# A row-wise softmax on one core: which tile is loaded first, and from which queue

## The chip, the cores and the metric

The kernel runs on one core of a Trainium2 chip. The time is device microseconds of one execution. The program has five instruction streams: PE (TensorE), DVE (VectorE), ACT (ScalarE), POOL (GpSimd) and SP (SyncE). Transfers between the chip's memory and the core's on-chip buffer are made by 16 DMA engines; SyncE, ScalarE and GpSimd each issue transfers on a queue of their own. "Issue" is the instruction that starts a transfer, "landing" the moment at which its semaphore is complete.

## The reference: softmax with temperature 2

```python
x = np.random.randn(16, 1024, 512).astype(np.float32)
x_scaled = x / 2.0
x_max = np.max(x_scaled, axis=-1, keepdims=True)
exp_x = np.exp(x_scaled - x_max)
out = (exp_x / np.sum(exp_x, axis=-1, keepdims=True)).astype(np.float32)
```

Input and output are 16,384 rows of 512 floats, 33.55 MB each. The kernel leaves the maximum out of its main path: it takes exp(0.5 x) and the row sums at once, multiplies by the reciprocal of the sum, and counts at the end whether all row sums lie between 1.0 and 1e30. Only if one does not, a second path (the `rounds`, L142) computes everything again with the maximum. With this input it does not run.

## The kernel before, in words

**Rows and tiles.** The 16,384 rows are spread over 128 partitions, so that each partition holds 128 rows of 2 KB ("rows" below are these 128). `TILES` (L10) cuts them into ten tiles, each given as (rows, place in the arena): 3, then 5, then eight of 15. A tile is one transfer in and one transfer out, and in memory each partition's part of a tile is contiguous: 15 rows are 30,720 bytes, 5 rows 10,240, 3 rows 6144. The arena (L49) is the on-chip buffer, with room for 98 of the 128 rows; the work is done in place.

**Loads.** SyncE issues tile 0 and ScalarE tile 1 in `early` (L153). Their instructions are moved by L278 to L286 in front of the barrier with which all engines begin. Tile 1 is the `SPREAD` tile: its fifth row goes by itself, in one transfer of partitions 0 to 125 and one of partitions 126 and 127 (L117), so that its load is three transfers. Behind the barrier ScalarE issues tiles 2 to 7 (`loads`, L157), one after the other on its queue. Tiles 8 and 9 reuse rows of the arena: `LATE` (L14) names the tiles whose stores must have landed first. GpSimd issues them (L176 to L179), after it has waited until all exponentials of the rows below `TURN` are done, and then for the stores in `LATE`, in order.

**Computing.** TensorE waits for each tile's landing and passes it on as permits, one for each chunk (L194). ScalarE takes a permit for a chunk and does one activation for each row of it, with the row's sum as a by-product. The first chunk (`HEAD`, three rows) is written out straight (L201); the others have five rows and run in a loop with a register as row number (`exponentials`, L259). VectorE then does a reciprocal and one multiply (L163 to L173) for up to three chunks of a tile, and for one chunk at a time in the last tile.

**Stores and the end.** SyncE issues the stores in the order of the tiles (L211), each when its multiplies are done. The store of the last tile but one has a semaphore of its own, `s_near`. The three computing engines wait for it and for the count of row sums, read the flag and step over the second path (L142 to L151). SyncE waits for `s_near` and for all the other stores (L256, L257), which ends the program.

Of the kernel before, what the change touches and what calls it, by code (L numbers as in the profile page):

```python
# [7 lines left out]


TILES = [  # L10
    (3, 0), (5, 3), (15, 8), (15, 23), (15, 38), (15, 53), (15, 68), (15, 83), (15, 0), (15, 15),
]

LATE = {8: (0, 1, 2), 9: (3,)}  # L14
ARENA = 98

HEAD = [3]
E = 5

SPREAD = 1  # L20

TURN = 83

LO, HI = 1.0, 1.0e30
G = 64
# [3 lines left out]
def kernel(  # L29
# [5 lines left out]
    nc = tc.nc  # L35
# [3 lines left out]
    Exp = mybir.ActivationFunctionType.Exp  # L39
# [6 lines left out]
    n_rows = N // P  # L46
    assert sum(r for r, _ in TILES) == n_rows

    arena = nc.alloc_sbuf_tensor("arena", (P, ARENA, D), fp32)  # L49
    stats = nc.alloc_sbuf_tensor("stats", (P, n_rows), fp32)  # L50
# [10 lines left out]
    for r, at in TILES:  # L61
        assert at == base % ARENA
        tiles.append((base, r, at))
# [6 lines left out]
    def sb(t):  # L70
        _, r, at = tiles[t]
        return arena[:, at : at + r, :]

    straight = sum(HEAD)
    sizes = HEAD + [E] * ((n_rows - straight) // E)
    starts = [sum(sizes[:k]) for k in range(len(sizes))]
    assert sum(sizes) == n_rows
    owner = [max(t for t, (b, _, _) in enumerate(tiles) if b <= s) for s in starts]
# [12 lines left out]
    ld = [nc.alloc_semaphore(f"ld{t}") for t in range(len(tiles))]  # L91
    s_home = {t: nc.alloc_semaphore(f"s_home{t}") for t in LATE}
    s_near = nc.alloc_semaphore("s_near")
    s_end = nc.alloc_semaphore("s_end")
    s_exp = nc.alloc_semaphore("s_exp")
    s_go = nc.alloc_semaphore("s_go")
# [16 lines left out]
    def load(eng, t):  # L113
        r = tiles[t][1]
        parts = [(0, P, 0, r)]
        if t == SPREAD:
            parts = [(0, P, 0, r - 1), (0, 126, r - 1, r), (126, P, r - 1, r)]  # L117
        for p, q, lo, hi in parts:
            eng.dma_start(  # L119
                out=sb(t)[p:q, lo:hi], in_=dram(xf, t)[p:q, lo:hi]  # L120
            ).then_inc(ld[t], 16)

    stored_by = {u: s_home[t] for t, us in LATE.items() for u in us}
    for t, (_, r, at) in enumerate(tiles):
        over = {u for u, (_, ru, au) in enumerate(tiles[:t]) if at < au + ru and au < at + r}
        assert over <= {u for v, us in LATE.items() if v <= t for u in us}

    def landings(ts):
        return 16 * len(list(ts))
# [9 lines left out]
    def take(eng, sem, n):  # L139
        eng.wait_ge(sem, n).then_inc(sem, -n)  # L140
# [11 lines left out]

    def early():  # L153
        load(nc.sync, 0)
        load(nc.scalar, 1)

    def loads():  # L157
        for t in range(2, min(LATE)):
            load(nc.scalar, t)

    def program():

        for j, ks in enumerate(pairs):  # L163
            b, c = starts[ks[0]], sum(sizes[k] for k in ks)
            a = b % ARENA
            nc.vector.reciprocal(  # L166
                out=recip[:, b : b + c], in_=stats[:, b : b + c]
            )._wait_ge(s_exp, ks[-1] + 1).then_inc(s_rec, 1)
            nc.vector.tensor_mul(  # L169
                out=arena[:, a : a + c],  # L170
                in0=arena[:, a : a + c],
                in1=recip[:, b : b + c].unsqueeze(2).to_broadcast([P, c, D]),
            )._wait_ge(s_rec, j + 1).then_inc(s_mul, 1)  # L173

        nc.gpsimd.memset(ones[:, :], 1.0).then_inc(s_ones, 1)  # L175
        nc.gpsimd.wait_ge(s_exp, starts.index(TURN))  # L176
        for t, us in LATE.items():
            nc.gpsimd.wait_ge(s_home[t], landings(us))
            load(nc.gpsimd, t)  # L179
        nc.gpsimd.tensor_scalar(  # L180
            out=inside[:, :], in0=stats[:, :], scalar1=LO, scalar2=HI,
            op0=Alu.max, op1=Alu.min,
        )._wait_ge(s_exp, len(sizes)).then_inc(s_cnt, 1)
        nc.vector.scalar_tensor_tensor(  # L184
            out=inside[:, :], in0=inside[:, :], scalar=1.0, in1=stats[:, :],
            op0=Alu.mult, op1=Alu.is_equal, accum_out=count[:, :],
        )._wait_ge(s_cnt, 1).then_inc(s_cnt, 1)
        nc.vector.tensor_scalar(  # L188
            out=flag[:, :], in0=total[:, :], scalar1=float(N), scalar2=None, op0=Alu.is_ge,
        )._wait_ge(s_tot, 1).then_inc(s_flag, 1)  # L190


        for t in range(len(tiles)):
            nc.tensor.wait_ge(ld[t], 48 if t == SPREAD else 16).then_inc(s_go, owner.count(t))  # L194
        nc.tensor.wait_ge(s_ones, 1)
        nc.tensor.matmul(  # L196
            total[:, :], lhsT=count[:, :], rhs=ones[:, :], start=True, stop=True
        )._wait_ge(s_cnt, 2).then_inc(s_tot, 1)

        nc.scalar.preload_act_table(Exp)  # L200
        for k, c in enumerate(HEAD):  # L201
            take(nc.scalar, s_go, 1)
            for b in range(starts[k], starts[k] + c):
                ins = nc.scalar.activation(  # L204
                    out=arena[:, b], in_=arena[:, b], func=Exp, scale=0.5,
                    accum_out=stats[:, b : b + 1],
                )
            ins.then_inc(s_exp, 1)
        exponentials(straight, n_rows)

        for t in range(len(tiles)):  # L211
            store(nc.sync, t)

        x_g = xf.rearrange("(t p r) d -> t p r d", p=P, r=G)
        o_g = of.rearrange("(t p r) d -> t p r d", p=P, r=G)
        data = arena[:, 0:G]

        def vector():  # L220
            for i in range(n_rows // G):
                nc.vector.reduce_max(
                    out=g_max[:, :], in_=data, axis=mybir.AxisListType.X, negate=True
                )._wait_ge(g_go, i + 1).then_inc(g_top, 1)
                nc.vector.reduce_sum(
                    out=g_sum[:, :], in_=data, axis=mybir.AxisListType.X
                )._wait_ge(g_exp, i + 1).then_inc(g_add, 1)
                nc.vector.reciprocal(
                    out=g_sum[:, :], in_=g_sum[:, :]
                )._wait_ge(g_add, i + 1).then_inc(g_rec, 1)  # L230

        def scalar():
            for i in range(n_rows // G):
                nc.scalar.activation(out=data, in_=data, func=Exp, scale=0.5)._wait_ge(
                    g_sub, i + 1
                ).then_inc(g_exp, 1)

        def gpsimd():
            nc.gpsimd.wait_ge(s_end, at_end)
            for i in range(n_rows // G):  # L240
                nc.gpsimd.dma_start(out=data, in_=x_g[i]).then_inc(g_ld, 16)
                nc.gpsimd.wait_ge(g_ld, 16 * (i + 1)).then_inc(g_go, 1)
                nc.gpsimd.tensor_add(
                    out=data, in0=data, in1=g_max[:, :].unsqueeze(2).to_broadcast([P, G, D])
                )._wait_ge(g_top, i + 1).then_inc(g_sub, 1)
                nc.gpsimd.tensor_mul(
                    out=data, in0=data, in1=g_sum[:, :].unsqueeze(2).to_broadcast([P, G, D])
                )._wait_ge(g_rec, i + 1).then_inc(g_mul, 1)
                nc.gpsimd.wait_ge(g_mul, i + 1)
                nc.gpsimd.dma_start(out=o_g[i], in_=data).then_inc(g_st, 16)  # L250
                nc.gpsimd.wait_ge(g_st, 16 * (i + 1))

        rounds(nc.vector, vector)
        rounds(nc.scalar, scalar)
        rounds(nc.gpsimd, gpsimd)
        nc.sync.wait_ge(s_near, 16)  # L256
        nc.sync.wait_ge(s_end, at_end)  # L257

    def exponentials(first, end):  # L259
        row = nc.scalar.alloc_register(f"row{first}")  # L260
        nc.scalar.reg_mov(row, first)
        with nc.scalar.While(lambda: nc.scalar.snap(row, min_val=first, max_val=end) < end):
            now = nc.scalar.snap(row, min_val=first, max_val=end - E)
            take(nc.scalar, s_go, 1)
            at = nc.s_assert_within(
                now % ARENA, 0, ARENA - E,
                skip_runtime_bounds_check_because="no chunk reaches over the arena's end",
            )
            for r in range(E):
                data = arena[:, r : ARENA - E + 1 + r][:, bass.ds(at, 1)]  # L270
                ins = nc.scalar.activation(  # L271
                    out=data, in_=data, func=Exp, scale=0.5,
                    accum_out=stats[:, r : n_rows - E + 1 + r][:, bass.ds(now, 1)],
                )
            ins.then_inc(s_exp, 1)
            nc.scalar.reg_add(row, row, E)
# [45 lines left out]
```

## Time and profile before

| what | value |
|---|---|
| runs | 159.97, 167.96 and 169.0 us; median 167.96 us |
| profiled execution: its own span, first to last instruction | 158.7 us |
| bytes moved in it, loads / stores | 33.55 / 33.55 MB |
| busy: ACT / DVE / POOL | 80.8 / 73.2 / 2.2 us |
| stores on SyncE's queue: first and last issue | 10.9 and 143.7 us |
| last landing | 158.7 us |

The profile shows one execution. A busy time is that of instructions which compute; waiting, branching and issuing transfers are not counted. A queue (q1 is SyncE's, q10 ScalarE's, q0 GpSimd's) is worked off by all 16 DMA engines in the order of issue, and the queues run beside one another. A line of stretches gives, for each engine, its busy time in that stretch with the number of instructions, then the DMA engines' mean busy share and the bytes moved per time. Packets are timed from start to end, and two that overlap on an engine both count, so a share can be a little over 1.

### The profile page before, as it was taken

How to read it: one execution, taken by the hardware profiler on the slowest of the kernel's cores; microseconds unless marked ns; L12 is line 12 of the kernel's file. 1: busy time of each engine (PE TensorE's matmuls, PEld its weight loads, DVE VectorE, ACT ScalarE, POOL GpSimd, SP SyncE). 2: the span in 40 equal slices, each digit the busy share in tenths (PEclk: the TensorE clock that was granted, in tenths of full speed). 3: DMA queues.
4: the chain of work that ended last, by engine and by line, in shares of the span. 5: the costliest groups of instructions: out<-in, count | busy, mean ns of one | idle time of the engine just before them, and what ended most of it. 6: DMA issues, size and time to landing. Idle time of an engine off the chain costs nothing. (4 is left out here: it accounts for less than half of the span.)

```text
span 158.7 us, 657 instructions
## 1 busy us (share of the span) xinstructions
PE 0.2 (0%) x2; PEld 0.1 (0%) x2; DVE 73.2 (46%) x27; ACT 80.8 (51%) x257; POOL 2.2 (1%) x8
## 2 busy tenths in 40 slices
PE   0000000000000000000000000000000000000000
PEld 0000000000000000000000000000000000000000
DVE  0047001992981990059500991008932981992000
ACT  0590598697498008940399001991597009940000
POOL 0000000000000000000000300000000000010000
DMA  7999998989999999999999999999999999999995
GB/s 271 382 496 396 463 437 324 480 382 485 410 457 410 457 410 449 418 449 418 441 426 441 426 434 434 426 441 426 441 418 449 418 449 410 457 403 465 403 457 256
DMA packets 3024, 67.11 MB, mean 423 GB/s; under 512 B 336, under 2 KB 336, under 8 KB 720
## 3 DMA queue, kind: packets, MB, share of 16 engines
q1 hardware_dynamic: 1584, 34.34, 50.4%
q10 hardware_dynamic: 1152, 24.90, 37.1%
q0 software_dynamic: 288, 7.86, 11.5%
HBM read 33.55 MB, written 33.55 MB: 423 GB/s over the span
## 5 line engine op out<-in xcount | busy, mean ns | idle before, releaser
L271 ACT ACTIVATE arena<-arena x125 | 76.8, 615 | 54.1 <-ACTq L140 54.1
L169 DVE TENSOR_TENSOR arena<-arena,recip 128x7680 f32<-128x7680 f32 (+2 forms) x12 | 70.2, 5847 | 0.4
L166 DVE RECIPROCAL recip<-stats 128x15 f32<-128x15 f32 (+2 forms) x12 | 2.7, 224 | 70.4 <-ACT arena L271 61.4
L271 ACT ACTIVATION_READ_ACCUMULATOR arena<-arena x125 | 23.4, 187 | 0.0
L200 ACT ACT_TABLE_LOAD x1 | 1.3, 1283 | 5.7 <-issue 5.7
L119 POOL DMA_DIRECT2D arena<-in_x_dram x2 | 1.3, 638 | 84.9 <-ACT arena L271 84.9
L204 ACT ACTIVATE arena<-arena 128x512 f32<-128x512 f32 x3 | 1.9, 619 | 0.0
L180 POOL TENSOR_SCALAR inside<-stats 128x128 f32<-128x128 f32 x1 | 0.6, 630 | 51.7 <-ACT arena L271 51.7
L204 ACT ACTIVATION_READ_ACCUMULATOR arena<-arena 128x1 f32 x3 | 0.6, 188 | 0.0
L196 PE MATMUL total<-ones,count 128*1 128x1 f32 x2 | 0.2, 164 | 143.9 <-DVE inside L184 143.9
L184 DVE SCALAR_TENSOR_TENSOR inside<-inside,stats 128x128 f32<-128x128 f32 x1 | 0.3, 282 | 0.0
L188 DVE TENSOR_SCALAR flag<-total 1x1 int32<-1x1 f32 x1 | 0.1, 146 | 0.3 <-PE total L196 0.3
L196 PEld LDWEIGHTS total<-ones,count 128*1 128x1 f32 x2 | 0.1, 80 | 143.9 <-DVE inside L184 143.9
L175 POOL MEMSET ones<- 128x1 f32 x1 | 0.1, 98 | 2.2 <-POOLq L37 2.2
L306 POOL MEMSET const-bfloat16-1.0<- 128x1 bf16 x1 | 0.1, 108 | 0.0
L306 POOL MEMSET const-uint8-127<- 128x1 uint8 x1 | 0.1, 108 | 0.0
L306 POOL MEMSET const-float32-0.0<- 128x1 f32 x1 | 0.1, 104 | 0.2 <-issue 0.2
L306 POOL MEMSET const-float32-1.0<- 128x1 f32 x1 | 0.1, 104 | 0.0
L184 DVE DVE_READ_ACCUMULATOR inside<-inside,stats 128x1 f32 x1 | 0.1, 80 | 0.0
## 6 DMA issues: line engine op xcount, KB each, us to landing
out_dram<-arena SPq DMA_DIRECT2D x8, 3840.0 KB, 26.2
arena<-in_x_dram ACTq DMA_DIRECT2D x6, 3840.0 KB, 46.7
arena<-in_x_dram POOLq DMA_DIRECT2D x2, 3840.0 KB, 33.6
out_dram<-arena SPq DMA_DIRECT2D x1, 1280.0 KB, 22.9
arena<-in_x_dram ACTq DMA_DIRECT2D x1, 1024.0 KB
arena<-in_x_dram SPq DMA_DIRECT2D x1, 768.0 KB, 5.6
out_dram<-arena SPq DMA_DIRECT2D x1, 768.0 KB, 14.6
arena<-in_x_dram ACTq DMA_DIRECT2D x1, 252.0 KB
```

The lines of the kernel that those rows point to most:

```text
L119: eng.dma_start(out=sb(t)[p:q, lo:hi], in_=dram(xf, t)[p:q, lo:hi]).then_inc(ld[t], 16)
L166: nc.vector.reciprocal(out=recip[:, b : b + c], in_=stats[:, b : b + c])._wait_ge(s_exp, ks[-1] + 1).then_inc(s_rec, 1)
L169: nc.vector.tensor_mul(out=arena[:, a : a + c], in0=arena[:, a : a + c], in1=recip[:, b : b + c].unsqueeze(2).to_broadcast([P, c, D]),)._w ...
L175: nc.gpsimd.memset(ones[:, :], 1.0).then_inc(s_ones, 1)
L180: nc.gpsimd.tensor_scalar(out=inside[:, :], in0=stats[:, :], scalar1=LO, scalar2=HI, op0=Alu.max, op1=Alu.min,)._wait_ge(s_exp, len(sizes) ...
L184: nc.vector.scalar_tensor_tensor(out=inside[:, :], in0=inside[:, :], scalar=1.0, in1=stats[:, :], op0=Alu.mult, op1=Alu.is_equal, accum_ou ...
L188: nc.vector.tensor_scalar(out=flag[:, :], in0=total[:, :], scalar1=float(N), scalar2=None, op0=Alu.is_ge,)._wait_ge(s_tot, 1).then_inc(s_f ...
L196: nc.tensor.matmul(total[:, :], lhsT=count[:, :], rhs=ones[:, :], start=True, stop=True)._wait_ge(s_cnt, 2).then_inc(s_tot, 1)
L200: nc.scalar.preload_act_table(Exp)
L204: ins = nc.scalar.activation(out=arena[:, b], in_=arena[:, b], func=Exp, scale=0.5, accum_out=stats[:, b : b + 1],)
L271: ins = nc.scalar.activation(out=data, in_=data, func=Exp, scale=0.5, accum_out=stats[:, r : n_rows - E + 1 + r][:, bass.ds(now, 1)],)
L306: nc = _bacc.Bacc("TRN2", target_bir_lowering=False, num_devices=1)
```

## The change

The order of the tiles changes, and with it who loads what:

- The tiles are now six of 15 rows, one of 5, two of 15 and one of 3. The arena has 95 rows instead of 98. There are ten tiles as before.
- SyncE still issues tile 0 in front of the barrier; this is now a tile of 15 rows. ScalarE issues nothing there. Tiles 1 to 6 are issued by ScalarE behind the barrier.
- No tile is split: `SPREAD` is `None`.
- GpSimd issues three late loads instead of two: tiles 7, 8 and 9, which wait for the stores of tiles 0, 1 and 2, one each. `TURN` is 80 instead of 83; both are row numbers, and row 80 stands behind the first chunk of tile 5.
- The chunk of three rows is the last one (`TAIL`) instead of the first; its activations are written out straight behind the loop. `s_near` now belongs to the last tile of 15 rows (tile 8), and the store behind it has 3 rows.

```diff
 TILES = [
-    (3, 0), (5, 3), (15, 8), (15, 23), (15, 38), (15, 53), (15, 68), (15, 83), (15, 0), (15, 15),
+    (15, 0), (15, 15), (15, 30), (15, 45), (15, 60), (15, 75), (5, 90), (15, 0), (15, 15), (3, 30),
 ]
-LATE = {8: (0, 1, 2), 9: (3,)}
-ARENA = 98
-HEAD = [3]
+LATE = {7: (0,), 8: (1,), 9: (2,)}
+ARENA = 95
+TAIL = 3
 E = 5
-SPREAD = 1
-TURN = 83
+SPREAD = None
+TURN = 80
...
-    straight = sum(HEAD)
-    sizes = HEAD + [E] * ((n_rows - straight) // E)
+    turned = n_rows - TAIL
+    sizes = [E] * (turned // E) + [TAIL]
...
     def early():
         load(nc.sync, 0)
-        load(nc.scalar, 1)
     def loads():
-        for t in range(2, min(LATE)):
+        for t in range(1, min(LATE)):
             load(nc.scalar, t)
...
         nc.scalar.preload_act_table(Exp)
-        for k, c in enumerate(HEAD):
-            take(nc.scalar, s_go, 1)
-            for b in range(starts[k], starts[k] + c):
-                ins = nc.scalar.activation(
-                    out=arena[:, b], in_=arena[:, b], func=Exp, scale=0.5,
-                    accum_out=stats[:, b : b + 1],
-                )
-            ins.then_inc(s_exp, 1)
-        exponentials(straight, n_rows)
+        exponentials(0, turned)
+        take(nc.scalar, s_go, 1)
+        for b in range(turned, n_rows):
+            a = b % ARENA
+            ins = nc.scalar.activation(
+                out=arena[:, a], in_=arena[:, a], func=Exp, scale=0.5,
+                accum_out=stats[:, b : b + 1],
+            )
+        ins.then_inc(s_exp, 1)
```

In the loop's body the slice of `stats` ends at the loop's own end instead of `n_rows`.

More of the change, by code (lines that the diff above doesn't have):

```diff
@@ L272, in exponentials @@
                     out=data, in_=data, func=Exp, scale=0.5,
-                    accum_out=stats[:, r : n_rows - E + 1 + r][:, bass.ds(now, 1)],
+                    accum_out=stats[:, r : end - E + 1 + r][:, bass.ds(now, 1)],
                 )
```

## The prediction

> **What bounds the kernel now.** I read the bandwidth slices of the page first, because a softmax over 33.6 MB touches each byte twice.
>
> ```profile
> span 158.7 us, 657 instructions
> ...
> DMA  7999998989999999999999999999999999999995
> GB/s 271 382 496 396 463 437 324 480 382 485 410 457 410 457 410 449 418 449 418 441 426 441 426 434 434 426 441 426 441 418 449 418 449 410 457 403 465 403 457 256
> DMA packets 3024, 67.11 MB, mean 423 GB/s; under 512 B 336, under 2 KB 336, under 8 KB 720
> ```
>
> The 16 DMA engines are busy in every slice but the first and the last. The same in stretches (columns: stretch, length, busy time of PE, PEld, DVE, ACT, POOL, clock, DMA share, GB/s):
>
> ```profile
> 0.00:1.00 1.00, 0.00 (x0) 0.00 (x0) 0.00 (x0) 0.00 (x0) 0.21 (x4) 1.00 0.00 0
> 1.00:10.00 9.00, 0.00 (x0) 0.00 (x0) 1.02 (x2) 4.32 (x11) 0.10 (x1) 1.00 1.03 397
> ...
> 40.00:100.00 60.00, 0.00 (x0) 0.00 (x0) 32.27 (x7) 29.41 (x95) 1.27 (x2) 1.00 1.00 433
> ...
> 130.00:157.00 27.00, 0.19 (x2) 0.09 (x2) 9.92 (x10) 9.31 (x30) 0.63 (x1) 1.00 1.01 436
> 157.00:159.00 2.00, 0.00 (x0) 0.00 (x0) 0.00 (x0) 0.00 (x0) 0.00 (x0) 1.00 0.04 15
> ```
>
> No byte moves in the first 1.0 us, then the share is 1.0 until 157, whether loads and stores mix (433 GB/s) or stores run alone (436). ACT and DVE work half the time. Then the waits of SyncE's queue, and the costliest groups kept apart by shape:
>
> ```profile
> SPq L137 <- DVE arena L169: 137.9, 10, 20.1
> SPq L257 <- DMA out_dram<-arena: 14.7, 1, 14.7
> ```
>
> ```profile
> L271 ACT ACTIVATE arena<-arena x125 | 76.8, 615 | 54.1 <-ACTq L140 54.1
> L169 DVE TENSOR_TENSOR arena<-arena,recip 128x7680 f32<-128x7680 f32 x7 | 57.1, 8158 | 0.2
> ```
>
> SyncE waits 137.9 us for multiplies to store, but with earlier stores in flight: that wait costs nothing. Its final 14.7 us (L257) is the last store being moved, while the chain of computing ended at 144.3. ACT in turn idles 54.1 us for loads. So the bound is the DMA engines, and a change counts only if it adds or removes bytes' time on them, leaves them idle, or lengthens the first 1.0 us or the last 1.1 us.
>
> **The price list.** From the trace's packet records: packets of 30,720 bytes (one partition of a 15-row tile) take 1138 ns at the median, on loads and stores alike; 10,240 bytes 385, 8192 bytes 309, 6144 bytes 234, 2048 bytes 84. Each engine has 8 packets per tile and direction. Before, per engine: 128 x 1.138 + 16 x 0.234 + 8 x 0.309 + 8 x 0.385 + 8 x 0.084 (mean) = 155.6 us. The last packets end near 157.6, so from 1.0 on 156.6 us pass, 1.0 above that floor. Packets longer than the median explain it: 0.37 us per engine at 6.5 us (the first 15-row load), 0.09 at 13.6 to 15, 0.38 at 24.7 to 27, 0.07 later. Landing of the last packet follows at 158.7.
>
> **Part 1, floor.** After, 128 x 1.138 + 16 x 0.385 (the five-row tile) + 16 x 0.234 (the three-row tile) = 155.6: a change of -0.06 us. Bytes are equal.
>
> **Part 2, start.** SyncE's load stays the first instruction; its first packets came 1.0 us after issue. Now it has 15 rows, so it alone covers 9.1 us, 1.0 to 10.1. ACT's three early issues (0.39 + 0.67 + 0.24 us) go. ACT was the last at the barrier with them (1.5 us), and the five-row load moves behind the barrier and behind five loads on ACT's queue. ACT's six remaining issues (0.36 to 0.56 us each) start between 1.5 and 2.7 us, and the nearest row for their way to the first packet is 1.0 (SyncE's) to 2.3 us (ACT's first). They are flowing by 5 us, well inside the 9.1: cost 0. If the longer first issue is slower (0.36 to 0.56 against 0.38), 0.2 is the upper end; 0 the lower.
>
> **Part 3, first results come late.** Two queues with work get 197 GB/s each in the packet records. Tile 0 alone from 1.0, then shared with tile 1 from about 3.3: 2 packets, then 6 x 2.28, so it lands at 17.1 (three rows landed at 5.6 before). A 15-row tile needed from landing to store 15 activations plus recip and multiply: landed 17.4, store issued 35.5. So the first store comes at 35.2 rather than 10.9. What covers this: 95 rows of loads need no store, 57.6 us of transfers. If they were not there the 24 us would be the price. ACT's later start (17.4 for 7.0) costs nothing either: 128 rows x 0.614 = 79 us, ACT had 54 us of idleness waiting on loads.
>
> **Part 4, the late loads and the end.** A 15-row store beside a load took 18.1 to 19.3 us in the trace, alone 9.1. By 37.4 tiles 0 to 3 are in. Paired: store 0 and load 4 end at 55.6, store 1 and load 5 at 73.8. TURN is now 80: POOL waits for the first chunk of tile 5, 77.3, and home store 1 is in at 73.8. Its issue took 5.0 us to its first packets (87.7 to 92.7), so tile 7 flows from 82.3; ACT's five-row load, whose 0.385 us packets alternate with 1.138 us store packets, lasts to about 87: no gap, and stores 2 to 4 are queued besides. POOL's third issue (tile 9) waits for store 2, near 87, and is needed only when tile 8 is in at 119; 0.6 us of POOL that nobody waits for. Tile 7 lands near 101, tile 8 near 119, tile 9 near 130. Store 7 runs until 144.9; store 8 is ready at 137.5 (119.4 + 18.1) and store 9 (three rows, DVE next in line, 2.0 us) at 139.5. The slack is 7.4 us; before, the last store was issued at 143.7 and the previous one landed at 149.6, 5.9. Cost 0, with both ends in the rival below. The flag check behind s_near took 1.33 us (149.57 to 150.89) and was covered by a 9.1 us store; its cover is now three rows, 8 x 0.234 = 1.87 us. Still covered; if the cover went it would cost up to 1.3.
>
> **Part 5, small packets and the split row.** The long packets at 13.6 and 24.7 to 27 came where small-packet stores met the loads; where a 15-row store met them (39.3) there was none. After, small packets meet others only with tiles 6 and 9. Bounds -0.47 (all gone) to +0.37 (one more like the first load's); I take -0.25, nearer to the 15-row contact. Without the split, the two engines that had no packet of that row get 8 x 0.084 = 0.67 us more, the 14 others 0.08 less. The last store's landings lie at 157.7 to 158.3 with one at 158.66, so the two may be the early ones (cost 0) or the late (0.6); I take 0.1.
> The Trainium skill (DMA: Bandwidth & Descriptors, "Why a DMA increments its semaphore by 16 and not by 1") says a copy uses the largest number of engines up to 16 that divides its partitions, so 126 run on 14 and 2 on 2. The trace agrees: that load's semaphore has 34 increments, 16 + 14 + 2 landings and two immediate ones at 1.30 and 1.67 us. The same page, "Latency and other measured facts", has engines 7 and 15 usually slower; by that rule the split was relief for a late engine and the sum would be +0.4 instead of -0.2. The landings, 0.36 us apart at most at the end, bear it out weakly.
>
> **Sum.** -0.06 + 0 + 0 + 0 - 0.25 + 0.1 = -0.2: span 158.5. The profiled execution's span is 158.7, and the fastest run, 159.97, stands 1.3 above it, so such an execution would be timed at 159.8. The median of the runs is 167.96, 8.0 above the fastest, with a third at 169.0. Nothing in the trace accounts for those 8 us. I take them as untouched by the change: a median of three like these is 167.96 - 0.2 = 167.8.
>
> **Rivals.** (a) Slower: a gap at the late loads. Place: store 8. If tile 8 lands more than 7.4 us after 119.4, SyncE's queue runs empty at 144.9 and each further us is lost. That needs POOL's packets at about 90 instead of 82. If POOL is held for one more paired transfer, 18.2 us, 10.8 are lost: 178.6. For: three loads now pass through POOL, each behind a store's landing, and 5.0 us of delay are shown. Against: margins of 3.5 us at home store 1 and 30 at store 2, and stores speed up when loads are absent, but that only brings the end of the queue nearer.
> (b) Faster: what lifts two of three runs by 8 us belongs to something that is removed (small packets among loads in the first 38 us, the 14- and 2-engine transfers). Then the median is 167.8 - 8.0 = 159.8. For: an 8 us spread that the trace of a 158.7 us execution cannot show. Against: all long packets together are 0.92 us here.
> (c) Nothing to see: relief or flag check exposed, the split 0.57 above what I took, the flag check 1.3, the first issue 0.2, the long packets 0.62 above: 170.5 at most; or the stalls at their lower end, 167.4 with the split at 0. Both stay within 2%.
>
> **How the numbers follow.** 2% (3.4 us) is about what a measurement of this kernel can tell from no change. Forecast with (c) 0.68, its own range 167.4 to 170.5; (b) 0.19, at 159.8, down to 158.7 if the other 0.67 us of long packets and the late landing (0.36 + 0.1) go with it; (a) 0.13. The range 158.7 to 170.5 takes in forecast and (b) and leaves out (a). Faster 0.19, same 0.68, slower 0.13.
>
> **What would show it.** Right: 2880 packets (320 under 512 B), the slices full from 1 us on, first store near 35, tile 0 in near 17, a DMA share of 1.0 up to the end, span 158 to 159. Part 4 is wrong if a stretch behind 120 us is below 0.95. Part 5's split is wrong if the last landing stands over 0.6 us behind the others. The forecast is wrong if the 30,720-byte packets no longer take 1138 ns, or if the 8 us of the other runs go with this change.

## The result, and the profile after

The changed kernel takes 161.53 us (median of five runs, 161.44 to 161.77), the kernel before 159.97: a ratio of 1.0103, 95% interval 1.0092 to 1.0114, that is 1.56 us between the two medians. Executions 2 to 9 us above the others of their kernel (167.96 and 169.0 here, 14 of 73 of before in all, three of six of e1 and one of six of e7) are left out of every ratio; the median shown ahead of the prediction was one of them, and no run shows where their extra time comes from. The profiled execution of the changed kernel was timed at 161.5, with a span of 160.2 (158.7 before).

The page after:

```profile
span 160.2 us, 651 instructions
...
DMA  7999999999899999999999999999999999999995
GB/s 261 460 414 445 430 437 445 422 437 407 361 414 460 414 445 422 430 445 399 460 402 448 391 430 422 445 422 460 414 453 425 417 442 388 455 445 422 453 402 216
DMA packets 2880, 67.11 MB, mean 419 GB/s; under 512 B 320, under 2 KB 320, under 8 KB 576
```

The bytes are the same, the packet counts are those forecast, and every slice but the two ends stands at 8 or 9 tenths, as before. Only the mean rate fell, 423 to 419 GB/s. The waits of SyncE's queue and the costliest groups after:

```profile
SPq L137 <- DVE arena L168: 138.6, 10, 35.4
SPq L256 <- DMA out_dram<-arena: 16.6, 1, 16.6
```

```profile
L270 ACT ACTIVATE arena<-arena x125 | 76.6, 613 | 49.9 <-ACTq L140 49.9
L168 DVE TENSOR_TENSOR arena<-arena,recip 128x7680 f32<-128x7680 f32 x8 | 65.3, 8158 | 0.3
```

The computing engines do the same work at the same speed (613 for 615 ns, 8158 for 8158), and the end is again a wait for stores, now 16.6 us. So the 1.5 us are inside the transfers. A line by stretches finds them. Before, in three stretches (the last figure of each line is GB/s, the one ahead of it the DMA share):

```profile
36.00:44.00 8.00, 0.00 (x0) 0.00 (x0) 5.36 (x2) 4.80 (x17) 0.00 (x0) 1.00 1.01 436
80.00:96.00 16.00, 0.00 (x0) 0.00 (x0) 8.41 (x2) 7.39 (x25) 1.27 (x2) 1.00 1.00 430
155.00:161.00 6.00, 0.00 (x0) 0.00 (x0) 0.00 (x0) 0.00 (x0) 0.00 (x0) 1.00 0.38 164
```

and after:

```profile
36.00:44.00 8.00, 0.00 (x0) 0.00 (x0) 7.22 (x3) 8.00 (x27) 0.00 (x0) 1.00 0.99 380
80.00:96.00 16.00, 0.00 (x0) 0.00 (x0) 10.98 (x4) 8.09 (x27) 0.91 (x2) 1.00 1.00 417
155.00:161.00 6.00, 0.00 (x0) 0.00 (x0) 0.00 (x0) 0.00 (x0) 0.00 (x0) 1.00 0.52 218
```

From 36 to 44 us, when the first store joins the loads, the share is 1.0 in both, yet the rate is 380 for 436 GB/s: the engines are busy all the time and move less. From 80 to 96, in which GpSimd's loads join (at 84 us after, at 93 before), it is 417 for 430. In the last stretch more is left to do.

The packet records say how. I add up what each packet took above the median of its size and divide by the 16 engines ("long packets", us per engine). I also list the 16 landings of the last store, which belong to the 16 engines:

```
                     long packets, us per engine          last store's landings, us
                     to 8 us   8 to 74   from 74   sum    first   median    last
before                 0.77      0.48      0.07    1.32   157.7   158.01   158.66
after                  0.69      0.92      0.53    2.15   158.2   158.80   160.10
```

The sum rose by 0.83 us, which is what the median landing moved (0.79). On top, the last landing stood 0.65 us behind the median before and 1.30 after. The two make the 1.44 us by which the last landing moved, and so nearly all of the 1.5 us of span. The records can be put together into 16 chains, one for each engine, since a packet nearly always begins within 10 ns of the end of the one before it. With 8 packets of every transfer in each chain, the 2560 data packets of the changed kernel come out as 16 chains of 160, and no chain has more than 0.2 us without a packet: no engine idles. The four chains that finish last lose 0.95 to 1.40 us between 80 and 96 us, the other twelve 0.7 or less. An engine that lost time does not get it back, because its 8 packets of every transfer stay its own, and the last store waits for the slowest.

### The profile page after: what moved, and what is told of

It reads as the page before. It is cut to its first block, busy times and chain, and to the rows that moved or that the text cites. A ratio compares the mean times of both kernels' runs of the same rounds, so it can differ in the third digit from the quotient of the medians.

```text
span 160.2 us, 651 instructions
## 1 busy us (share of the span) xinstructions
PE 0.2 (0%) x2; PEld 0.1 (0%) x2; DVE 72.4 (45%) x23; ACT 80.4 (50%) x257; POOL 7.5 (5%) x9
## 2 busy tenths in 40 slices
DMA packets 2880, 67.11 MB, mean 419 GB/s; under 512 B 320, under 2 KB 320, under 8 KB 576
## 5 line engine op out<-in xcount | busy, mean ns | idle before, releaser
L179 POOL TENSOR_SCALAR inside<-stats 128x128 f32<-128x128 f32 x1 | 5.4, 5412 | 41.4 <-ACT arena L204 41.4
L119 POOL DMA_DIRECT2D arena<-in_x_dram x3 | 1.8, 600 | 91.6 <-ACT arena L270 77.6
## 6 DMA issues: line engine op xcount, KB each, us to landing
out_dram<-arena SPq DMA_DIRECT2D x8, 3840.0 KB, 35.1
arena<-in_x_dram ACTq DMA_DIRECT2D x5, 3840.0 KB, 36.8
arena<-in_x_dram SPq DMA_DIRECT2D x1, 3840.0 KB, 18.7
```

The source lines that it names most:

```text
L119: eng.dma_start(out=sb(t)[p:q, lo:hi], in_=dram(xf, t)[p:q, lo:hi]).then_inc(ld[t], 16)
L179: nc.gpsimd.tensor_scalar(out=inside[:, :], in0=stats[:, :], scalar1=LO, scalar2=HI, op0=Alu.max, op1=Alu.min,)._wait_ge(s_exp, len(sizes) ...
```

## The experiments

Three theories stood at the start. **A**: the split row had relieved two late engines. **B**: the loss is made where a store of 15 rows first meets the loads ("the contact" below); its price follows the size of the store's packets. **C**: three queues at work at once make the second loss. Later ones are named where they come. All ratios are to the kernel before on the same chip; none reaches 2%, so they are read by their intervals. Long packets and landings are those of one profiled execution each. Nine runs below and the change load tile 0 alike, as one transfer of 15 rows, and their long packets to 8 us lie between 0.59 and 0.78: a difference of 0.1 in these columns says nothing.

```
                            ratio, 95% interval        profiled   long packets, us per engine   landings of last store
                                                       run, us    to 8   8 to 74  from 74       first to last, us
e1  before, unsplit         1.0046 (1.0015, 1.0077)    160.16     0.38    0.88    0.27          1.05
e2  after, split            1.0137 (1.0124, 1.0150)    161.92     0.75    0.97    0.85          2.43
e3  store 0 as 5+5+5        1.0031 (1.0004, 1.0058)    159.99     0.59    0.69    0.02          0.85
e4  TURN 90                 1.0116 (1.0102, 1.0129)    161.53     0.78    0.97    0.92          1.29
e5  store 0 as 3+12         1.0081 (1.0066, 1.0097)    160.94     0.69    0.80    0.28          1.58
e6  store 0 as 12+3         1.0059 (1.0043, 1.0075)    160.70     0.67    0.97    0.13          1.38
e7  five rows first         1.0054 (1.0040, 1.0067)    160.72     0.64    0.92    0.28          1.46
e8  three rows in middle    1.0096 (1.0082, 1.0110)    161.16     0.69    0.90    0.34          1.81
e9  before, big store first 1.0069 (1.0051, 1.0087)    161.58     0.84    0.51    0.50          1.87
e10 store 0 as 1+2+4+8      1.0021 (1.0012, 1.0030)    160.39     0.67    0.77    0.04          1.01
e11 e3, load 0 as 5+5+5     1.0031 (1.0006, 1.0055)    160.12     0.67    0.52    0.07          0.87
e12 late loads by ScalarE   1.0157 (1.0141, 1.0173)    162.34     0.68    0.77    0.58          3.09
e13 e12 and e3              1.0023 (1.0005, 1.0041)    160.19     0.64    0.69    0.03          0.88
e14 before, by ScalarE      0.9997 (0.9987, 1.0006)    159.86     0.71    0.42    0.04          0.68
```

**e1 and e2, the split.** In the kernel before, and the other way round in the changed one:

```diff
-SPREAD = 1
+SPREAD = None
```

> The kernel before without the split of the fifth row of tile 1, everything else as it was. Theory A (the end is set by the last engine, and the split gave two engines 0.67 us less work): about +0.6 us on 159.97, 160.5 to 160.7, with two landings of the last store standing 0.5 us or more behind the rest. Theory B (the lost time of the change is in packets that take longer where a store of 15 rows first meets loads, and where GpSimd's loads join): within 0.15 us of before.

> The changed kernel with the last row of tile 1 split as before (126 and 2 partitions; its other packets then have 28,672 bytes). Theory A: about -0.6 us, near 160.9. Theory B: the long packets stay (2.1 us per engine) and the time stays at 161.4 to 161.7; at most 0.2 is gained if the two relieved engines happen to be the late ones.

Taking the split out of before costs 0.46% (0.7 us, with an interval from 0.2 to 1.2): near A's 0.6. The figure stands on three executions, though, of 160.16, 160.17 and 161.51 us, and the profiled one is the first. In it no two landings stand behind the rest; nine of the 16 are about 0.7 us later than the other seven, after long packets of 0.88 us per engine in the middle for 0.48. Putting it into the changed kernel makes that slower, 1.0137 for 1.0103, with 0.48 us per engine of new long packets at 18 to 21 us, where the small packets run between big ones. The contact at 36 to 44 us then costs only 0.20 us per engine (0.87 in the change), and the later loss grows to 0.85 (0.53). If relief of two engines were the matter, e2 had to gain. A is out as the cause of the change's loss. That the split serves the kernel before is likely from three executions, and how is not shown.
The Trainium skill (DMA: Bandwidth & Descriptors, "Latency and other measured facts") has engines 7 and 15 usually slower; by that, relief should have helped in both. Here four engines are late after, and e2 loses, so that rule alone does not account for this case; the packet records name no engine, so whether those two are among the late ones can't be seen.

**e3, the first store in three parts**, at the same moment (e5, e6 and e10 differ in the list):

```diff
+PARTS = {0: [(0, 5), (5, 10), (10, 15)]}
...
-        eng.dma_start(out=dram(of, t), in_=sb(t)).then_inc(sem_of.get(t, s_end), 16)
+        for lo, hi in PARTS.get(t, [(0, r)]):
+            eng.dma_start(
+                out=dram(of, t)[:, lo:hi], in_=sb(t)[:, lo:hi]
+            ).then_inc(sem_of.get(t, s_end), 16)
```

> The changed kernel with the first store as three transfers of five rows (10,240 bytes a packet instead of 30,720), at the same moment. Theory B, with a price that grows with the store's packet (0.08 us per engine for 6144 bytes, 0.39 for 10,240, 0.87 for 30,720): the long packets at 38 to 42 us fall from 0.87 to about 0.4 us per engine, the time by about 0.4 to 161.1. Rival (the price is that of any first store beside loads, or of the moment, whatever its packets): 0.87 stays, time 161.5.

This one edit takes back most of the loss, 1.0031 for 1.0103, and more than the 0.4 us that B had expected. (One of its six executions took 161.62 us, as long as the change, and so did two of twelve in e11, 161.7 and 161.8; they are in the ratios, and no trace shows such a one.) Its stretches:

```profile
36.00:44.00 8.00, 0.00 (x0) 0.00 (x0) 7.23 (x3) 8.00 (x27) 0.00 (x0) 1.00 1.01 417
80.00:96.00 16.00, 0.00 (x0) 0.00 (x0) 5.68 (x3) 1.97 (x7) 0.54 (x1) 1.00 1.00 430
155.00:161.00 6.00, 0.00 (x0) 0.00 (x0) 0.00 (x0) 0.00 (x0) 0.00 (x0) 1.00 0.34 141
```

The contact costs less (417 for 380 GB/s, 0.33 us per engine for 0.87 at 36 to 44), but another 0.35 follows before 74 us, and the larger part of the gain is that the second loss is gone (430 GB/s, 0.02 us) and the engines end within 0.85 us of one another. The edit touches nothing but the first store, so what happens there decides, by whatever way, what happens 45 us later.

**e4, when GpSimd's loads join.**

```diff
-TURN = 80
+TURN = 90
```

> The changed kernel with TURN 90: GpSimd issues the late loads when all exponentials of tiles 0 to 5 are done, near 85 us instead of 79, so that they join when ScalarE's queue is empty (89 us). Theory C (the 0.5 us per engine of long packets at 82 to 94, up to 1.4 on six engines, come from three queues at work at once, and make the late engines): long packets there nearly vanish, the last landing falls by 0.7 to 1.0 us, 160.5 to 160.9. Rival (they come from the joining of GpSimd's queue itself): they stay, a few us later, 161.4 to 161.7.

ScalarE's last load had landed at 87.4 us and GpSimd's first packets began at 90.2, so there were never three at once; the long packets are still there (0.92 us per engine, two thirds of them at 102 to 108), and the ratio stays near that of the change, 1.0116. C falls. Its rival, that GpSimd's joining makes the loss, had the time right; e12 puts it aside.

**e5 and e6, the same two parts in both orders.** The list is `[(0, 3), (3, 15)]` and `[(0, 12), (12, 15)]`.

> The changed kernel with the first store as two transfers, first 3 rows (6144 bytes a packet), then 12 (24,576). Theory B (the price of first contact follows the first packets' size): long packets at 38 to 42 us at 0.1 to 0.45 us per engine, time 160.0 to 160.6. Rival R (it was not the contact that made three parts fast, but that small store packets leave the loads more of the engines, so that ScalarE's queue was empty before GpSimd's loads joined): here only 8 small packets go first, ScalarE's queue ends near 83 us as GpSimd's begins, and the time stays above 161.0.

> The same two transfers in the other order, 12 rows first (24,576 bytes), then 3. Theory B: long packets at 38 to 42 us at 0.6 to 0.9 us per engine, time 161.0 to 161.6, and 0.5 us or more above the order 3, 12. Rival R: the same time as with 3 first, within 0.2 us, since bytes and packets are the same.

Three rows first is the slower order, if anything: B's forecast of 0.5 us the other way is out. Of R's two forecasts the time above 161.0 came in for e5 (161.17 us), and equal times did not (160.80 in e6). At the contact itself the packets did go with size (e6 0.96 us per engine from 36 to 44; e5 0.28 from 40 to 48 and 0.49 more when its 24,576-byte packets began at 50 to 54), but the sum is close, and the later loss and the spread decide the time. Both recover only a part.

**e7 and e8, which half of the change.** e7 puts the small tile first and keeps the change's tail; e8 keeps the change's start and has the tail of before.

```diff
-    (15, 0), (15, 15), (15, 30), (15, 45), (15, 60), (15, 75), (5, 90), (15, 0), (15, 15), (3, 30),
+    (5, 0), (15, 5), (15, 20), (15, 35), (15, 50), (15, 65), (15, 80), (15, 0), (15, 15), (3, 30),
```

```diff
-    (15, 0), (15, 15), (15, 30), (15, 45), (15, 60), (15, 75), (5, 90), (15, 0), (15, 15), (3, 30),
+    (15, 0), (15, 15), (15, 30), (15, 45), (15, 60), (15, 75), (5, 90), (3, 95), (15, 0), (15, 15),
```

> The change with the five-row tile first instead of seventh (5, six of 15, two of 15, 3): SyncE's early load has 5 rows, the first store has 10,240 bytes a packet and comes near 17 us; the tail with three late loads and the three-row tile at the end is that of the change. Theory B: long packets near 20 us at about 0.4 us per engine, time 159.9 to 160.5. Rival T (the tail costs it: three loads by GpSimd, the last store of three rows): 161.3 to 161.7 as with the change.

> The change's start with the end of before: six tiles of 15, 5, 3, then two late tiles of 15 (98 rows in the arena, two loads by GpSimd, the last store has 15 rows). Theory B: the first contact is that of a 15-row store as in the change, 0.8 us per engine or more at 38 to 42 us, time 161.0 to 161.7. Rival T: 159.8 to 160.3.

With before's tail the loss stays (1.0096 for 1.0103): three loads by GpSimd and a last store of three rows cost nothing that can be seen. With the small tile first half of it is gone (1.0054). So the loss is made by the start. e7 missed its range of 159.9 to 160.5 by a little (160.72), and its first contact, before 20 us, cost 0.62 us per engine where B had 0.4: one small tile ahead does not do what the two of before do.

**e9, the suspected cost added to the kernel before.**

```diff
-        for t in range(len(tiles)):
+        for t in [2, 0, 1, *range(3, len(tiles))]:
             store(nc.sync, t)
```

> The kernel before with one thing added: SyncE stores tile 2 (15 rows) first and tiles 0 and 1 (3 and 5 rows) behind it, so that the first store is at 35 us with packets of 30,720 bytes as in the change. Loads, tail and GpSimd's two loads are those of before. Theory B2 (the price is that of the step in the store's packet size: 0.8 to 0.95 us per engine from nothing to 24 or 30 KB, about 0.4 from 6 to 10 KB, 0 from 10 to 30 KB; the spread of the engines that it leaves then costs at the ends of later stores and at the last landing): long packets at 36 to 42 us of 0.8 us per engine or more, time 160.8 to 161.6. Rival H (it is the loads of the head, or the tail, and the store only shows it): 159.7 to 160.2 as before.

A first store of 15 rows at 35 us makes the kernel before slower by 0.69%, most of what the whole change did, with loads, split and tail as they were: rival H is out. But B2 misses too. The contact cost 0.42 us per engine, not 0.8; what grew is the later loss, 0.50 us per engine for 0.07. Its stretches:

```profile
36.00:44.00 8.00, 0.00 (x0) 0.00 (x0) 7.97 (x2) 8.00 (x27) 0.00 (x0) 1.00 1.03 422
80.00:96.00 16.00, 0.00 (x0) 0.00 (x0) 10.54 (x3) 5.35 (x18) 0.54 (x1) 1.00 1.02 426
155.00:161.00 6.00, 0.00 (x0) 0.00 (x0) 0.00 (x0) 0.00 (x0) 0.00 (x0) 1.00 0.42 179
```

In the chains one engine lost 1.5 us at 80 to 96 and ended its packets at 159.86, when the other 15 were done by 158.42. One engine out of 16 made the time of this execution, which is the slowest of six (160.50 to 161.58 us).
The edit does two things at once: the first store is bigger, and it is later, 35.1 us instead of 10.9. Lateness alone is not the price, since e3 and e10 keep a late first store (36.8 us) and lose 0.2 to 0.3%.

**e10 and e11, small packets further.** e10 has `[(0, 1), (1, 3), (3, 7), (7, 15)]`; e11 is e3 with SyncE's first load in three parts as well:

```diff
-        parts = [(0, P, 0, r)]
+        parts = [(0, P, lo, hi) for lo, hi in PARTS.get(t, [(0, r)])]
```

> The changed kernel with the first store in four transfers of 1, 2, 4 and 8 rows (2048, 4096, 8192, 16,384 bytes a packet). Theory B2: small steps, so that the contacts together cost 0.2 to 0.6 us per engine and the last landings stand within 1.0 us: 159.9 to 160.5. Rival R (what made three parts of five rows fast is that 24 small packets let ScalarE's queue run empty by 69 us, before GpSimd's loads): here 24 small packets of 7 us in all go first and the next step, to 30 KB, is as before; the time is then near that of the order 3, 12, 161.0 to 161.5.

> The changed kernel with the first store and also SyncE's first load in three transfers of five rows. The first packets on an idle memory path took 0.6 us per engine longer than 1138 ns with 30,720 bytes and 0.25 (plus 0.37 when the 15-row loads began) in the kernel before. If that price too follows the packet, the long packets of the first 6 us fall from 0.6 to 0.3 us per engine and the time lies 0.2 to 0.4 under that with the store alone in parts: 159.7 to 160.0. If not, 160.0 to 160.3.

e10 is as good as e3 (1.0021), and rival R's 161.0 to 161.5 is out in its form. B2 had the time, but not the reason: the long packets in the middle are 0.77 us per engine, over its 0.2 to 0.6 and not far under the 0.92 of the change, only later (0.01 of them at 36 to 44). What is gone is the later loss (0.04) and with it the spread. In e3, e10, e11 and e13 the load packets of tiles 1 to 6 were through by 68.7 us, and the first store packets of 30,720 bytes began at 69; in e5 and e6 big store packets ran beside them. That fits R in another form: what helps would be that big stores never meet these loads. The kernel before speaks against it, with 30,720-byte stores beside such loads from 39 us on and no loss, but there smaller stores had gone ahead, and no run separates the two. In e11 the first packets cost what the whole transfer's cost, 0.67 us per engine for 0.69: that price did not follow the packet here.

**e12, e13 and e14, another queue for the late loads.** ScalarE issues them between its exponentials (in e14 tiles 8 and 9 behind row 82):

```diff
-        nc.gpsimd.wait_ge(s_exp, starts.index(TURN))
-        for t, us in LATE.items():
-            nc.gpsimd.wait_ge(s_home[t], landings(us))
-            load(nc.gpsimd, t)
...
-        exponentials(0, turned)
+        exponentials(0, TURN)
+        late(7)
+        late(8)
+        exponentials(TURN, ARENA)
+        late(9)
+        exponentials(ARENA, turned)
```

> The changed kernel with tiles 7, 8 and 9 issued by ScalarE between its exponentials (7 and 8 behind row 79, 9 behind row 94) instead of by GpSimd. Theory J (the loss at 82 to 94 us comes with GpSimd's queue as a third one): no long packets there, the last landing at most 1.1 us behind the first, time 160.3 to 160.8, with the first contact of 0.8 to 0.9 us per engine left. Rival K (it comes from how stores and loads meet once the engines are out of step): 0.3 us per engine or more of long packets behind 70 us, time 161.2 to 161.7.

> The same with the first store in three transfers of five rows. Theory J and K alike: no second loss, as with the three parts alone; 159.8 to 160.2. Over 160.5 would say that ScalarE's queue brings a loss of its own.

> The kernel before with tiles 8 and 9 issued by ScalarE behind row 82. There is no second loss in it to remove (0.05 us per engine): 159.7 to 160.0 under J and K. Below 159.6 would say that GpSimd's queue costs it too.

Theory J is out, and e12 overshoots K's range: without GpSimd's queue the loss is there (0.58 us per engine), and it falls on fewer engines. In the chains three of them lose 1.8 to 2.2 us between 80 and 96 us, and these three end last, so the spread is 3.1 us and the kernel the slowest of all. Its stretches:

```profile
36.00:44.00 8.00, 0.00 (x0) 0.00 (x0) 7.22 (x3) 8.00 (x27) 0.00 (x0) 1.00 0.99 388
80.00:96.00 16.00, 0.00 (x0) 0.00 (x0) 10.91 (x4) 8.16 (x27) 0.00 (x0) 1.00 1.00 418
155.00:161.00 6.00, 0.00 (x0) 0.00 (x0) 0.00 (x0) 0.00 (x0) 0.00 (x0) 1.00 0.47 198
```

The same edit beside a first store in parts (e13) or in the kernel before (e14) is harmless. That is the cleanest pair of the study: e12 and e13 differ in nothing but the parts of one store, and stand at 1.0157 and 1.0023.
The Trainium skill (DMA: Bandwidth & Descriptors, "Issuing engines are not separate DMA queues") says that transfers run on the same 16 DMA engines whichever engine starts them, and that issuing from several saves only issue time. e14 (0.9997) agrees, and so do e3 and e13 (1.0031 and 1.0023). e12 and the change (1.0157 and 1.0103) differ, so beside a whole first store the queue is not without effect; no run shows how.

No version beat both kernels; e14 equals the kernel before, and e3, e10, e11 and e13 stand 0.2 to 0.3% above it.

**What is shown and what stays open.** Shown: the loss is in packets that take longer on busy engines and in engines that end apart; a single 15-row store as the first one brings most of it (taken out in e3, e10, e11, e13; put in with e9); the split, the tail, TURN and GpSimd's queue do not. Open: why a packet takes longer when a store joins, why a second loss follows 45 us later in some kernels, and which engines it hits. Packet size alone does not give it (e5, e6, e9), and the packet records name no engine. Nor does the price of the contact: 0.20 us per engine at 36 to 44 was followed by 0.85 in e2, 0.96 by 0.13 in e6.

## Why the prediction was wrong, by its own steps

- **What bounds the kernel: right.** The DMA engines bound both, and neither computing engine mattered. Its list of long packets was short, though: it has 0.92 us per engine for before, the records 1.32. What it left out lies in the first packets, up to 6 us.
- **Part 1, floor: right.** Same bytes, 2880 packets, the median of the 30,720-byte packets still 1138 ns.
- **Part 2, start: right.** First packets again at 1.0 us. ScalarE's first issue came at 1.44 and its packets at 5.2, inside the cover of 9.1 us.
- **Part 3, late first results: cost 0, right.** Tile 0 landed at 18.7 (17.1 forecast), the first store was issued at 36.8 (35.2). The 197 GB/s for each of two queues does not fit the 2.28 us for two packets, which the landing was worked out from and which make 216.
- **Part 4, end: right.** GpSimd's packets began at 84.1 (82.3 forecast). Store 8 was issued at 141.3 with the store ahead of it landing at 149.2: a slack of 7.9 us for 7.4. The flag check ran from 158.3 to 159.0 and was over before the last landing at 160.1. Rival (a), a gap there, did not come.
- **Part 5: the step that failed.** It took -0.25 us for the long packets, because where a 15-row store met the loads (39.3) there had been none. That row was of another situation: at 39.3 in before two smaller stores had gone ahead on the same queue. Met for the first time by a 15-row store, the sum of long packets rose by 0.83 us. By stretches that is -0.08 to 8 us, +0.44 from 8 to 74 and +0.46 behind. The upper bound of +0.37 was the price of a first load, and a second loss was in no row. The 0.1 taken for the late landing was mis-sized and put down to the split; it was 0.65, from engines that long packets had set apart, and e2 shows that the split would not have mended it.
- **The sum** of -0.2 us on the profiled execution's own time (159.8) thus missed by 1.7: 1.08 in the long packets, 0.55 in the last landing.
- **The median.** 167.8 was built on a median of 167.96 that comes from executions left out of the ratio above, so it forecast a level and not the effect. The range held 161.53 only because rival (b) stretched it down to 158.7, for a gain that did not come: that was luck. The 0.68 for a time within 2% was right, and within it the sign was wrong.

## What to carry to other kernels

When 16 DMA engines are the bound and busy all the time, read the rate and the landings of the last store beside the share: a share of 1.0 with fewer GB/s is time lost, and the slowest engine sets the end. The order in which the first transfers of a queue join another queue's traffic can be worth 1% even where bytes and idle time stay the same. Letting the first store join in three or four small transfers was worth 0.7 to 0.8% here (e3, e10); in two, of 3 and 12 rows, only 0.2% (e5). A price read from one contact holds for that contact only: look at what stood on the same queue ahead of it.

## What the runs showed of the hardware that was not expected

- A packet of 30,720 bytes that takes 1138 ns at the median took up to 2066 ns when the first store joined (38 to 42 us), and up to 1911 ns once more at 82 to 93, on engines with no idle time.
- The first packets of an execution are long, and smaller ones did not reliably help: to 8 us, 0.67 us per engine with 10,240-byte parts (e11), 0.69 with 30,720 bytes (after), 0.38 with 6144 and 10,240 on two queues (e1).
- GpSimd's check of the row sums (L179, before L180) took 5.4 us after and 0.63 before; no run shows why. It lies beside other work in both.
- From GpSimd's issue to its first packets 5.0 us passed in both kernels (79.1 to 84.1, 87.7 to 92.7).
